# Layer norms of a one-layer encoder: transposes directly behind the normalisation, gain and bias applied per partition, rows of the residual scaled later

## The chip, the cores and the metric

The kernel runs on one core of a Trainium2 chip. The metric is the device time of one execution in microseconds (us). Engines are named as the profile names them: PE multiplies matrices (PEld loads its stationary operand), DVE works on tensors elementwise, ACT applies functions and copies, POOL does slow elementwise work and issues accumulating DMAs, SP issues the other DMAs. Each engine runs its own instructions in order and waits on semaphores of the others.

## The reference

One layer over 256 tokens of width 2048, all in float32:

```python
x = _layer_norm(ALPHA * x + 0.5 * _swiglu(x, ffn1_w1, ffn1_w3, ffn1_w2), ln1_g, ln1_b)
mix = _hybrid_mixer(x, w_in, b_gates_m, conv_m, norm_m, w_up_m, w_up_sb, w_out)
x = _layer_norm(ALPHA * x + mix, ln2_g, ln2_b)
x = _layer_norm(ALPHA * x + 0.5 * _swiglu(x, ffn2_w1, ffn2_w3, ffn2_w2), ln3_g, ln3_b)
x = x + sigmoid(x @ w_ple_gate) * (p @ w_ple_proj)
```

`_layer_norm` takes mean and variance over the 2048 columns of a token, and returns `(x - mu) * rsqrt(var + eps) * g + b`. The feed-forward width is 5632. The mixer is a projection to about 11,000 columns, two attention-like branches, gates and an output projection.

## The kernel before

Tokens stand in two halves, t = 0 and t = 1, of 128 rows each; the residual is kept as two tiles `xres0` and `xres1` of 128x2048. Products take activations transposed (columns on the partitions), in tiles `actT` for a chunk c of 512 columns and a half t. Every float32 operand is held as a rounded part and a remainder, and a product is three matmuls: rounded by rounded, rounded by remainder (of the weight), remainder (of the activation) by rounded. Lines 1061, 1062 and 1063 are those three; only the last needs the remainder of the activation.

Weights come in tiles of 256x512 (`raw`, 512 KB). ACT rounds each into `split` (L1010), DVE subtracts for the remainder (L1014). How many split tiles may exist at once is a number: 5 in the feed-forward stages, 6 in the mixer, and 11 around the borders between stages (`SPLIT_EDGE`, within `EDGE` tiles of a border). A **unit** is a weight tile used for one half t: six matmuls. Usually both halves use a tile one after the other. Around the three norms the order is skewed: the last `SKEW` tiles ahead of a norm are first used all for t = 0, then all for t = 1, and the first `SKEW` tiles behind it likewise. So a split tile lives until its unit of t = 1.

The engine orders are what this program emits, since it is written out by a small planner at build time: `sched.now` advances by each unit's matmul time, a generator spawned with a delay emits its instructions once the clock has passed, and nothing is reordered later. PSUM has a ring of six banks (`ps`) for products and transposes.

A norm goes so. A group's last unit adds its product to `xres` on DVE (L497 in the feed-forward stages, L875 in the mixer) and takes statistics of these 512 columns (L391). When all four are there, `finish` aggregates them (L397), takes the root on ACT and its reciprocal on DVE (L400), and for each chunk normalises (L404), multiplies by g (L406) and adds b (L407), both broadcast over the rows and held in four pages. `turn` follows 5.0 planner-us behind: four transposes on PE (L266), the rounding copy out of PSUM on ACT (L268), and the remainder on DVE (L274). For the second norm the kernel also keeps an unrounded copy (L273), from which `form_turn` builds sums for the next stage, and scales the rows by ALPHA on POOL (L421).

Of the kernel before, what the change touches and what calls it, by code (L numbers as in the profile page):

```python
# [21 lines left out]
ALPHA = 2.0 ** 0.25  # L22
EPS = 1e-5
COL = 512

PAGES = 44
TEMP_BUFS = 6
FORMED = 8
SPARE = 2
# [151 lines left out]
def kernel(  # L181
# [6 lines left out]
    nc = tc.nc  # L188
    x, out = x[0], out[0]
# [7 lines left out]
    small = ctx.enter_context(tc.tile_pool(name="small", bufs=4))  # L197
# [38 lines left out]
    def activate(out, in_, func, **kw):  # L236
        use_table(func)
        nc.scalar.activation(out, in_, func, **kw)  # L238
# [4 lines left out]
    ident = consts.tile([P, P], F32, name="ident")  # L243
# [6 lines left out]
    xres = [res_pool.tile([P, D], F32, name=f"xres{t}") for t in range(TT)]  # L250
# [8 lines left out]
    def split_psum(hi, lo, ps):  # L259
        nc.scalar.copy(hi, ps)  # L260
        nc.vector.tensor_tensor(out=lo, in0=ps, in1=hi, op=ALU.subtract)

    def transposed(src, act, c, t):
        ps = misc([P, 4, P])
        for k in range(4):
            nc.tensor.transpose(ps[:, k], src[:, k * P:(k + 1) * P], ident[:])  # L266
        dst = act.get(c, t)
        nc.scalar.copy(dst[:, 0], ps[:])  # L268
        if act.forms:
            if c not in act.whole:  # L270
                act.whole[c] = big()
                pages[0] += 1
            nc.scalar.copy(act.whole[c][:, t * COL:(t + 1) * COL], ps.rearrange("q k s -> q (k s)"))  # L273
        nc.vector.tensor_tensor(out=dst[:, 1], in0=ps[:], in1=dst[:, 0], op=ALU.subtract)  # L274
        act.mark(c, t, 4)
        if act.forms and all(act.ready(c, h) for h in range(TT)):
            sched.spawn(form_turn(act, c), DELAY["form"] + 3.0 * c)
# [95 lines left out]


    class Norm:
        def __init__(self, g, b, act, after):
            self.g_in, self.b_in, self.act, self.after = g, b, act, after
            self.stats, self.half = {}, {}

        def load(self):  # L380
            use_table(ACT.Sqrt)
            self.g, self.b = [big(), big()], [big(), big()]
            for k in range(2):
                ks = slice(k * 1024, (k + 1) * 1024)
                nc.sync.dma_start(out=self.g[k][:], in_=self.g_in[ks].partition_broadcast(P))
                nc.sync.dma_start(out=self.b[k][:], in_=self.b_in[ks].partition_broadcast(P))

        def chunk(self, t, c):
            if t not in self.stats:
# [5 lines left out]
        def finish(self, t):  # L395
            mv = small.tile([P, 2], F32, name="mv", tag="mv")
            nc.vector.bn_aggr(out=mv[:], in_=self.stats[t][:])  # L397
            rstd = small.tile([P, 1], F32, name="rstd", tag="rstd")
            activate(rstd[:], mv[:, 1:2], ACT.Sqrt, bias=eps[:, 0:1])
            nc.vector.reciprocal(out=rstd[:], in_=rstd[:])  # L400
            for c in range(4):
                xs = xres[t][:, c * COL:(c + 1) * COL]
                gs = slice((c % 2) * COL, (c % 2 + 1) * COL)
                nc.vector.tensor_scalar(out=xs, in0=xs, scalar1=mv[:, 0:1], scalar2=rstd[:, 0:1],  # L404
                                        op0=ALU.subtract, op1=ALU.mult)
                nc.vector.tensor_tensor(out=xs, in0=xs, in1=self.g[c // 2][:, gs], op=ALU.mult)  # L406
                nc.vector.tensor_tensor(out=xs, in0=xs, in1=self.b[c // 2][:, gs], op=ALU.add)  # L407
                sched.spawn(self.turn(t, c), DELAY["ln_turn"])
                yield DELAY["ln_step"]

        def turn(self, t, c):
            xs = xres[t][:, c * COL:(c + 1) * COL]
            transposed(xs, self.act, c, t)
            if self.after:
                yield DELAY["after"]
                self.after(xs)
            return
            yield

    def scaled(xs):  # L420
        nc.gpsimd.tensor_scalar(out=xs, in0=xs, scalar1=ALPHA, scalar2=None, op0=ALU.mult)  # L421
# [537 lines left out]
    splits = {}  # L959
    pos = {"load": 0, "split": 0, "at": 0, "raw": 0}  # L960

    def mixing():
        j = pos["split"]
        return any(-EDGE <= j - e < EDGE for e, _ in edges) or [m for e, m in edges if e <= j][-1:] == [True]

    def limits(j):

        if any(-EDGE <= j - e < EDGE for e, _ in edges):
            return RAW_EDGE, SPLIT_EDGE
        mixer = [m for e, m in edges if e <= j][-1:] == [True]  # L970
        return (RAW_MIX, SPLIT_MIX) if mixer else (RAW_FFN, SPLIT_FFN)
# [129 lines left out]
```

## Time and profile before

| | |
|---|---|
| median of three runs | 2219.58 us (2218.72 to 2219.68) |
| the profiled execution | 2219.43 us, of which the span of its instructions 2217.6 us |
| granted PE clock, mean | 0.998 |
| places of the norms in the span | about 690 to 720, 1400 to 1430, 2094 to 2125 us |

The span is what the hardware profiler saw from the first to the last instruction; 1.8 us of the time lie around it. A row of the timeline gives start, duration, engine, line, operation, output and inputs, shapes, and in brackets how long the engine stood still before it and what ended that. The view of waits adds these brackets up. A row of the windows gives, for a stretch of the span, its length and then the busy time and number of instructions of PE, PEld, DVE, ACT and POOL, the granted clock, the share of the DMA engines and GB/s. Rows of grouped instructions give shape, count, busy time in us and the mean of one in ns.

### The profile page before, as it was taken

The page shows a single profiled execution, that of the slowest core. Times are in us where ns is not written, and L with a number is a line of the kernel's source. Part 1 is how long each engine was busy: PE and PEld are TensorE (multiplying, and loading weights), DVE is VectorE, ACT ScalarE, POOL GpSimd, SP SyncE. Part 2 cuts the span into 40 slices and gives each one's busy share as a digit, 9 for nine tenths or more (in the row PEclk, how much of TensorE's full clock was granted, in tenths as well). Part 3 has the DMA queues.
Part 4 walks back from the last instruction along what each step waited for, and adds up shares of the span by engine and source line. Part 5 has one row for each costly group of instructions (what it writes and reads, how often), then busy time and mean ns, then how long its engine had stood idle before and what let it go on. Part 6 is the DMA issues. An engine that isn't in the chain of part 4 may idle for free.

```text
span 2217.6 us, 27467 instructions
## 1 busy us (share of the span) xinstructions
PE 2198.4 (99%) x10065; PEld 1822.2 (82%) x10065; DVE 1688.1 (76%) x1856; ACT 1236.2 (56%) x1441; POOL 201.4 (9%) x175
## 2 busy tenths in 40 slices
PE   9999999999999999999999999999999999999999
PEld 7888888888887888888888888788888888888878
DVE  6889988888799674654445456789898989889874
ACT  6556656666563655545643344466666666666452
POOL 3111011110100000100100000121011101110000
PEclk9999999999999999999999999999999999999999
DMA  9899889987991765655566666679879988899543
GB/s 346 219 255 269 252 249 288 276 247 215 271 363 55 224 182 170 181 170 163 161 188 185 189 224 219 228 171 284 252 235 246 306 253 250 243 276 301 188 160 96
DMA packets 262857, 501.83 MB, mean 226 GB/s; under 512 B 15745, under 2 KB 24769, under 8 KB 262721
## 3 DMA queue, kind: packets, MB, share of 16 engines
q1 hardware_dynamic: 227904, 432.95, 59.0%
q0 software_dynamic: 34816, 67.12, 16.9%
q8 instruction: 79, 1.29, 0.2%
q14 instruction: 58, 0.47, 0.1%
HBM read 497.91 MB, written 2.10 MB: 225 GB/s over the span
## 4 chain that ended last, share of the span: by engine, by line
PE 95%; DVE 3%; DMA 1%; issue 1%; ACT 0%; DVEq 0%; ACTq 0%
PE mm L1063 27%; PE mm L1062 27%; PE mm L1061 27%; PE seeded L1063 4%; PE seeded L1062 4%; PE seeded L1061 4%; PE ms L266 1%; DMA raw<-in_ffn_w_dram 1%; DVE xres L406 1%; DVE split L1014 0%; DVE xres L404 0%; DVE xres L407 0%; DVE actT L274 0%; DVE stats L391 0%; PE ms L772 0%
## 5 line engine op out<-in xcount | busy, mean ns | idle before, releaser
L1014 DVE TENSOR_TENSOR split<-raw,split 128x1024 fp32r<-128x1024 f32 (+1 forms) x1013 | 1181.1, 1202 | 302.1 <-ACT split L1010 289.5
L1010 ACT CAST split<-raw 128x1024 fp32r<-128x1024 f32 (+1 forms) x1013 | 1017.6, 1038 | 448.2 <-PE mm L1062 112.4
L1061 PE MATMUL mm<-split,actT 128*128 128x512 f32 (+2 forms) x2768 | 1076.5, 389 | 0.3 <-ACT split L1010 0.3
L1063 PE MATMUL mm<-split,actT 128*128 128x512 f32 (+2 forms) x2768 | 1066.4, 385 | 8.2 <-DVE actT L274 8.2
L1062 PE MATMUL mm<-split,actT 128*128 128x512 f32 (+2 forms) x2768 | 1065.5, 385 | 1.8 <-DVE split L1014 1.8
L1063 PEld LDWEIGHTS mm<-split,actT 128*128 128x128 f32 x2768 | 520.7, 188 | 115.0 <-DVE actT L274 11.4
L1062 PEld LDWEIGHTS mm<-split,actT 128*128 128x128 f32 x2768 | 521.2, 188 | 103.1 <-DVE split L1014 3.0
L1061 PEld LDWEIGHTS mm<-split,actT 128*128 128x128 f32 x2768 | 521.0, 188 | 102.2 <-issue 1.3
L330 POOL DMA_DIRECT2D raw<-in_ffn_w_dram x128 | 155.5, 1219 | 982.6 <-DVE split L1014 787.5
L335 DVE TENSOR_TENSOR raw<-raw 128x1024 f32<-128x1024 f32 x128 | 155.6, 1216 | 11.0 <-DMA raw<-in_ffn_w_dram 11.0
L1061 PE MATMUL seeded<-split,actT 128*128 128x512 f32 x384 | 150.5, 392 | 0.0
L1062 PE MATMUL seeded<-split,actT 128*128 128x512 f32 x384 | 149.6, 390 | 0.0
L1063 PE MATMUL seeded<-split,actT 128*128 128x512 f32 x384 | 149.5, 389 | 0.0
L497 DVE SCALAR_TENSOR_TENSOR xres<-mm,xres 128x512 f32<-128x512 f32 x160 | 108.4, 682 | 12.8 <-PE mm L1063 12.8
L268 ACT CAST actT<-ms 128x512 fp32r<-128x512 f32 x84 | 49.1, 588 | 113.8 <-PE ms L266 113.7
L1062 PEld LDWEIGHTS seeded<-split,actT 128*128 128x128 f32 x384 | 72.1, 188 | 15.0 <-DVE split L1014 0.4
L1063 PEld LDWEIGHTS seeded<-split,actT 128*128 128x128 f32 x384 | 72.1, 188 | 15.0
L1061 PEld LDWEIGHTS seeded<-split,actT 128*128 128x128 f32 x384 | 72.1, 188 | 14.7
L274 DVE TENSOR_TENSOR actT<-ms,actT 128x512 fp32r<-128x512 f32 x84 | 57.1, 684 | 30.0 <-ACT actT L268 17.7
L421 POOL TENSOR_SCALAR xres<-xres 128x512 f32<-128x512 f32 x16 | 27.0, 1692 | 325.2 <-DVE xres L404 300.5
L238 ACT ACTIVATE temp<-mm 128x512 f32<-128x512 f32 (+1 forms) x38 | 21.8, 574 | 58.0 <-PE mm L1063 58.0
L238 ACT ACTIVATE big<-mm 128x512 f32<-128x512 f32 x20 | 12.0, 598 | 55.8 <-PE mm L1063 55.8
(124 smaller groups left out, 630.6 us busy)
## 6 DMA issues: line engine op xcount, KB each, us to landing
raw<-in_ffn_w_dram SPq DMA_DIRECT2D x527, 512.0 KB, 8.0
raw<-in_w_in_dram SPq DMA_DIRECT2D x168, 512.0 KB, 3.7
raw<-in_ffn_w_dram POOLq DMA_DIRECT2D x128, 512.0 KB, 9.5
raw<-in_w_out_dram SPq DMA_DIRECT2D x32, 512.0 KB, 5.2
raw<-in_w_ple_gate_dram SPq DMA_DIRECT2D x24, 512.0 KB, 4.9
raw<-in_w_up_m_dram SPq DMA_DIRECT2D x16, 512.0 KB, 4.1
raw<-in_w_up_sb_dram SPq DMA_DIRECT2D x16, 512.0 KB, 4.1
raw<-in_w_ple_gate_dram SPq DMA_DIRECT2D x16, 256.0 KB, 4.6
```

The lines of the kernel that those rows point to most:

```text
L238: nc.scalar.activation(out, in_, func, **kw)
L268: nc.scalar.copy(dst[:, 0], ps[:])
L274: nc.vector.tensor_tensor(out=dst[:, 1], in0=ps[:], in1=dst[:, 0], op=ALU.subtract)
L330: nc.gpsimd.dma_start(out=raw.tile[:, :, :cols], in_=src.src, accum_op=ALU.add)
L335: nc.vector.tensor_tensor(out=a.tile[:, :, :cols], in0=a.tile[:, :, :cols], in1=b.tile[:, :, :cols], op=ALU.add)
L421: nc.gpsimd.tensor_scalar(out=xs, in0=xs, scalar1=ALPHA, scalar2=None, op0=ALU.mult)
L497: nc.vector.scalar_tensor_tensor(out=xs, in0=ps, scalar=0.5, in1=xs, op0=ALU.mult, op1=ALU.add)
L1010: nc.scalar.copy(hi[:, ks], r[:, ks])
L1014: nc.vector.tensor_tensor(out=lo[:, ks], in0=r[:, ks], in1=hi[:, ks], op=ALU.subtract)
L1061: nc.tensor.matmul(ps, hi, w[0][:, k, :u.cols], start=first, stop=False, skip_group_check=u.onto)
L1062: nc.tensor.matmul(ps, hi, w[1][:, k, :u.cols], start=False, stop=False, skip_group_check=u.onto)
L1063: nc.tensor.matmul(ps, lo, w[0][:, k, :u.cols], start=False, stop=last, skip_group_check=u.onto)
```

## The change

`finish` only normalises (L425, once L404), and emits the chunks 0.7 instead of 1.7 planner-us apart. `turn` comes 3.4 behind instead of 5.0: four transposes of the normalised rows (L434), and behind them g and b as scalars per partition, out of PSUM: one of the four 128x128 blocks on DVE (L439), three on ACT (through L238). The result, in SBUF, is then rounded on ACT (L260) and its remainder taken on DVE (L261). g and b per partition (`gb`) come from two small DMAs, one transpose and one copy (L405). The rows of the residual get g and b later, in `rows` (L460, L461, or L463 and L465 with ALPHA in them for the second norm, whose POOL scaling goes away), two DVE operations per chunk and half. `SKEW` and `EDGE` go from 6 to 8, the four broadcast pages are counted, and the rule for loading ahead looks at the split tiles that exist.

```diff
-EDGE = 6
+EDGE = 8
-SKEW = 6
+SKEW = 8
-    "after": 14.0, "form": 14.0, "ln_turn": 5.0, "ln_step": 1.7, "h": 8.0, "silu": 6.0, "late": 9.0, "rest": 1.2, "mt": 3.2,
+    "gb": 12.0, "form": 14.0, "ln_turn": 3.4, "ln_step": 0.7, "h": 8.0, "silu": 6.0, "late": 9.0, "rest": 1.2, "mt": 3.2,
         def load(self):
...
+            raw = temp()
+            n = D // P
+            nc.sync.dma_start(out=raw[0:n, 0:P], in_=self.g_in.rearrange("(c q) -> c q", q=P))
+            nc.sync.dma_start(out=raw[n:2 * n, 0:P], in_=self.b_in.rearrange("(c q) -> c q", q=P))
+            sched.spawn(self.columns(raw, n), DELAY["gb"])
...
                 nc.vector.tensor_scalar(out=xs, in0=xs, scalar1=mv[:, 0:1], scalar2=rstd[:, 0:1],
                                         op0=ALU.subtract, op1=ALU.mult)
-                nc.vector.tensor_tensor(out=xs, in0=xs, in1=self.g[c // 2][:, gs], op=ALU.mult)
-                nc.vector.tensor_tensor(out=xs, in0=xs, in1=self.b[c // 2][:, gs], op=ALU.add)
                 sched.spawn(self.turn(t, c), DELAY["ln_turn"])
         def turn(self, t, c):
-            xs = xres[t][:, c * COL:(c + 1) * COL]
-            transposed(xs, self.act, c, t)
-            if self.after:
-                yield DELAY["after"]
-                self.after(xs)
+            act = self.act
+            ps = misc([P, 4, P])
+            for k in range(4):
+                nc.tensor.transpose(ps[:, k], xres[t][:, (4 * c + k) * P:(4 * c + k + 1) * P], ident[:])
+            y = whole(act, c, t) if act.forms else temp()[:]
+            for k in (3, 0, 1, 2):
+                yk, gk, bk = y[:, k * P:(k + 1) * P], *(self.gb[:, i, 4 * c + k:4 * c + k + 1] for i in range(2))
+                if k == 3:
+                    nc.vector.tensor_scalar(out=yk, in0=ps[:, k], scalar1=gk, scalar2=bk, op0=ALU.mult, op1=ALU.add)
+                else:
+                    activate(yk, ps[:, k], ACT.Identity, scale=gk, bias=bk)
+            dst = act.get(c, t)
+            split_psum(dst[:, 0], dst[:, 1], y.rearrange("q (k s) -> q k s", s=P))
...
+            self.left -= 1
+            if self.left == 0:
+                sched.spawn(self.rows(), self.delay)
+        def rows(self):
+            for c in range(4):
+                for t in range(TT):
...
+                    if self.alpha is None:
+                        nc.vector.tensor_tensor(out=xs, in0=xs, in1=g, op=ALU.mult)
+                        nc.vector.tensor_tensor(out=xs, in0=xs, in1=b, op=ALU.add)
+                    else:
+                        nc.vector.scalar_tensor_tensor(out=xs, in0=xs, scalar=self.alpha, in1=g,
+                                                       op0=ALU.mult, op1=ALU.mult)
+                        nc.vector.scalar_tensor_tensor(out=xs, in0=b, scalar=self.alpha, in1=xs,
+                                                       op0=ALU.mult, op1=ALU.add)
+                    yield self.step
...
-    norm1 = Norm(ln1_g[0], ln1_b[0], x1T, None)
+    norm1 = Norm(ln1_g[0], ln1_b[0], x1T, None, 30.0, 6.0)
-    norm2 = Norm(ln2_g[0], ln2_b[0], x2T, scaled)
+    norm2 = Norm(ln2_g[0], ln2_b[0], x2T, ALPHA, 24.0, 5.0)
-    norm3 = Norm(ln3_g[0], ln3_b[0], x3T, None)
+    norm3 = Norm(ln3_g[0], ln3_b[0], x3T, None, 6.0, 2.6)
...
-               and (mixing() or pages[0] + pos["raw"] + 2 * limits(pos["split"])[1] < PAGES - SPARE)):
+               and (mixing() or pages[0] + pos["raw"] + 2 * max(limits(pos["split"])[1], len(splits)) < PAGES - SPARE)):
```

What this does to the engine orders is shown at the first norm; the other two read alike. First DVE before, from the first normalised chunk of t = 0 (`xres0`) on; `big` are the broadcast g and b, `mm` products, `ms` transposes.

```order
L404 TENSOR_SCALAR xres0_86<-xres0_86,mv_5821,rstd_5823 128x512
L406 TENSOR_TENSOR xres0_86<-xres0_86,big_5520 128x512
L407 TENSOR_TENSOR xres0_86<-xres0_86,big_5522 128x512
L1014 TENSOR_TENSOR split_5838<-raw_5556,split_5837 128x1024
L497 SCALAR_TENSOR_TENSOR xres1_87<-mm_5830,xres1_87 128x512
L391 BN_STATS stats_5770<-xres1_87 128x6
L404 TENSOR_SCALAR xres0_86<-xres0_86,mv_5821,rstd_5823 128x512
L406 TENSOR_TENSOR xres0_86<-xres0_86,big_5520 128x512
L407 TENSOR_TENSOR xres0_86<-xres0_86,big_5522 128x512
L497 SCALAR_TENSOR_TENSOR xres1_87<-mm_5856,xres1_87 128x512
```

And DVE of the changed kernel from the fourth normalised chunk of t = 0 on; `temp` is the transposed chunk with g and b, `gb` their values per partition.

```order
L425 TENSOR_SCALAR xres0_86<-xres0_86,mv_5800,rstd_5802 128x512
L439 TENSOR_SCALAR temp_5850<-ms_5845,gb_5668 128x128
L261 TENSOR_TENSOR actT_5855<-temp_5850,actT_5855 128x512
L1065 TENSOR_TENSOR split_5859<-raw_5559,split_5858 128x1024
L548 SCALAR_TENSOR_TENSOR xres1_87<-mm_5837,xres1_87 128x512
L413 BN_STATS stats_5828<-xres1_87 128x6
L439 TENSOR_SCALAR temp_5877<-ms_5872,gb_5668 128x128
L261 TENSOR_TENSOR actT_5882<-temp_5877,actT_5882 128x512
L1065 TENSOR_TENSOR split_5886<-raw_5581,split_5885 128x1024
L439 TENSOR_SCALAR temp_5903<-ms_5898,gb_5668 128x128
```

The broadcast g and b are gone from here. In their place each chunk has L439 and, directly behind it, L261; between the chunks stand splits of weight tiles (L1065, once L1014), of which the order before has one at this place. The adds and statistics of t = 1 stand behind them as before. From the add that completes `xres0` to the first normalised chunk of t = 1, DVE now has five splits, all four turns of t = 0, and four adds with statistics of t = 1, in this order.

ACT of the changed kernel at the same place, with the semaphores that each row waits for.

```order
L1061 CAST split_5831<-raw_5517 128x1024 [waits DMAHW5_49]
L238 ACTIVATE temp_5850<-ms_5845,gb_5668 128x128 [waits DVE_49]
L238 ACTIVATE temp_5850<-ms_5845,gb_5668 128x128 x2
L260 CAST actT_5855<-temp_5850 128x512 [waits Activation_49]
L1061 CAST split_5858<-raw_5559 128x1024 [waits DMAHW7_49]
L238 ACTIVATE temp_5877<-ms_5872,gb_5668 128x128 [waits DVE_49]
```

The first of the three ACTIVATEs of a chunk waits for DVE: for L439 of the same chunk, which reads the same PSUM bank. The CAST follows them, and L261 on DVE needs that CAST; the next weight tile's CAST stands behind it.

PE of the changed kernel where the first transpose of t = 1 stands: the end of the third unit behind the norm, and the fourth.

```order
L1114 MATMUL mm_5961<-split_5735,actT_5882 128x512 [waits DVE_49]
L1112 MATMUL mm_5961<-split_5735,actT_5882 128x512
L1113 MATMUL mm_5961<-split_5736,actT_5882 128x512
L1114 MATMUL mm_5961<-split_5735,actT_5882 128x512
L434 MATMUL ms_5983<-ident_82,xres1_87 128x128 [waits DVE_49]
L434 MATMUL ms_5983<-ident_82,xres1_87 128x128 x3
L1112 MATMUL mm_5961<-split_5815,actT_5882 128x512
L1113 MATMUL mm_5961<-split_5816,actT_5882 128x512
```

Between the last unit of `xres0` and this transpose PE has 8 units of t = 1, the four transposes of t = 0, and 3 units behind the norm. Before, the first transpose of t = 1 stood 4 units behind the norm, the last half having 6 units. The transpose waits for DVE's first L425 of t = 1, and every later PE row stands behind it.

More of the change, by code (lines that the diff above doesn't have):

```diff
@@ L269, in transposed, with whole, finished @@
         if act.forms:
[L270 to L273, printed above, removed]
+            nc.scalar.copy(whole(act, c, t), ps.rearrange("q k s -> q (k s)"))
         nc.vector.tensor_tensor(out=dst[:, 1], in0=ps[:], in1=dst[:, 0], op=ALU.subtract)
+        finished(act, c, t)
+    def whole(act, c, t):
+        if c not in act.whole:
+            act.whole[c] = big()
+            pages[0] += 1
+        return act.whole[c][:, t * COL:(t + 1) * COL]
+    def finished(act, c, t):
         act.mark(c, t, 4)
@@ L375, with __init__ @@
     class Norm:
-        def __init__(self, g, b, act, after):
-            self.g_in, self.b_in, self.act, self.after = g, b, act, after
-            self.stats, self.half = {}, {}
+        def __init__(self, g, b, act, alpha, delay, step):
+            self.g_in, self.b_in, self.act = g, b, act
+            self.alpha, self.delay, self.step = alpha, delay, step
+            self.stats, self.left = {}, 8
         def load(self):
@@ L382, in load @@
             self.g, self.b = [big(), big()], [big(), big()]
+            pages[0] += 4
             for k in range(2):
@@ L386, in load, with columns @@
                 nc.sync.dma_start(out=self.b[k][:], in_=self.b_in[ks].partition_broadcast(P))
+            raw = temp()
[3 more added lines that the diff above has]
+            sched.spawn(self.columns(raw, n), DELAY["gb"])
+        def columns(self, raw, n):
+            ps = misc([P, 2 * n])
+            nc.tensor.transpose(ps[:], raw[0:2 * n, 0:P], ident[0:2 * n, 0:2 * n])
+            self.gb = small.tile([P, 2, n], F32, name="gb", tag="gb", bufs=1)
+            nc.vector.tensor_copy(out=self.gb[:], in_=ps.rearrange("q (a c) -> q a c", c=n))
+            drop()
+            return
+            yield
         def chunk(self, t, c):
```

8 lines of the change are left out of this document (7 added, 1 removed).

## The prediction

> **What bounds the kernel now.** I read the page first, then PE's waits, then the windows around the norms, then the timelines of DVE and PE there.
>
> ```profile
> span 2217.6 us, 27467 instructions
> PE 2198.4 (99%) x10065; PEld 1822.2 (82%) x10065; DVE 1688.1 (76%) x1856; ACT 1236.2 (56%) x1441; POOL 201.4 (9%) x175
> PE mm L1063 <- DVE actT L274: 8.2, 7, 2.7
> PE ms L266 <- ACT split L1010: 2.2, 1, 2.2
> 690.00:720.00 30.00, 26.84 (x121) 21.24 (x120) 27.29 (x47) 5.90 (x10) 0.00 (x0) 0.94 0.18 46
> 1400.00:1430.00 30.00, 27.14 (x131) 21.54 (x131) 24.86 (x40) 9.70 (x19) 10.55 (x6) 1.00 0.61 216
> 2094.00:2125.00 31.00, 27.94 (x128) 22.16 (x127) 28.49 (x47) 12.26 (x22) 0.00 (x0) 0.94 0.36 103
> ```
>
> PE is busy for 99% of the span: whatever PE doesn't wait for costs nothing. Of its 19 us of idle time nearly half lies at the three norms (the windows, first number behind the length): 3.16, 2.86 and 3.06, together 9.1 us. In the first and third the granted clock is 0.94, which is another 0.06 x 26.84 = 1.6 and 0.06 x 27.94 = 1.7. So the norms cost **12.4 us now**, and that is the most that this change can win. DVE is busy for 27.29 of 30 there: it is DVE's queue that PE waits for.
>
> **The walk along DVE.** This is DVE at the first norm; 692.73 is the add that completes `xres0`, and PE ended that half's last matmul just before (call it T0).
>
> ```profile
> 692.73 0.69 DVE L497 SCALAR_TENSOR_TENSOR xres<-mm,xres 128x512 f32<-128x512 f32 x1 [1.16 <-PE mm L1063]
> 693.45 0.69 DVE L391 BATCH_NORM_STATS2 stats<-xres 128x6 f32<-128x512 f32 x1
> ...
> 694.80 0.16 DVE L400 RECIPROCAL rstd<-rstd 128x1 f32<-128x1 f32 x1 [0.36 <-ACT rstd L238]
> 695.00 0.55 DVE L404 TENSOR_SCALAR xres<-xres,mv,rstd 128x512 f32<-128x512 f32 x1
> 695.58 0.69 DVE L406 TENSOR_TENSOR xres<-xres,big 128x512 f32<-128x512 f32 x1
> 696.31 0.69 DVE L407 TENSOR_TENSOR xres<-xres,big 128x512 f32<-128x512 f32 x1
> 696.92 1.22 DVE L1014 TENSOR_TENSOR split<-raw,split 128x1024 fp32r<-128x1024 f32 x1
> 698.05 0.68 DVE L497 SCALAR_TENSOR_TENSOR xres<-mm,xres 128x512 f32<-128x512 f32 x1
> 698.77 0.69 DVE L391 BATCH_NORM_STATS2 stats<-xres 128x6 f32<-128x512 f32 x1
> 699.38 0.53 DVE L404 TENSOR_SCALAR xres<-xres,mv,rstd 128x512 f32<-128x512 f32 x1
> ```
>
> Start to start: add to first normalised chunk 2.27 (the head of a norm); a split 1.13; an add with its statistics 1.33; L406 and L407 together 1.34 a chunk, which the change takes off this place; a 128x512 operation that another follows 0.61. DVE stood idle for 1.16 ahead of T0, so it enters the norm without a backlog, and I assume the same behind the change.
>
> **What a turn costs DVE now.** A chunk had L274 here, 0.61 of DVE. The new turn is L439 and L261 next to each other, and between them lies ACT's whole part, because the first ACTIVATE waits for L439 and L261 waits for the CAST. No row shows L439, nor an ACTIVATE of 128x128 with two pointers out of PSUM; the nearest are these.
>
> ```profile
> L261 DVE TENSOR_TENSOR actT<-ms,actT 128x128 fp32r<-128x128 f32 x16 | 4.6, 290 | 14.8 <-ACT actT L260 14.8
> L238 ACT ACTIVATE temp<-ms,aT 128x128 f32<-128x128 f32 x4 | 1.4, 360 | 0.0
> L238 ACT ACTIVATE temp<-ms,cw 128x256 f32<-128x256 f32 x16 | 7.6, 474 | 18.4 <-DVE temp L671 14.6 <-PE ms L660 3.8
> L260 ACT CAST actT<-temp 128x512 fp32r<-128x512 f32 x16 | 9.3, 621 | 8.3 <-DVE split L1014 3.4 <-PE mm L1063 1.7 <-PE mm L1062 1.6
> 1112.03 0.27 ACT L260 CAST actT<-ms 128x128 fp32r<-128x128 f32 x1 [3.15 <-PE ms L795]
> 1112.33 0.29 DVE L261 TENSOR_TENSOR actT<-ms,actT 128x128 fp32r<-128x128 f32 x1 [2.00 <-ACT actT L260]
> 1112.65 0.43 ACT L260 CAST actT<-ms 128x128 fp32r<-128x128 f32 x2 [0.36 <-DVE actT L261]
> ```
>
> The hand-off between ACT and DVE is 1112.30 to 1112.33, so 0.03. I take 0.29 for L439; 3 x 0.36 = 1.08 for the ACTIVATEs (the row of the same engine, shape and source, without overlap, since theirs has one pointer operand less); 0.62 for the CAST; three hand-offs; 0.61 for L261: **2.69 us of DVE for a turn**. From below: ACTIVATEs that overlap like the two small CASTs, which take 0.43 together (0.16 + 0.16 + 0.27 = 0.59), with 0.21 for L439: about 2.1. From above: 3 x 0.474 = 1.42 and 0.46 for L439, an estimate at the length of half a chunk: about 3.2 with L261 at its full 0.69.
>
> [...]
>
> **The sum at an edge.** DVE from T0 to the end of the first normalised chunk of t = 1, by the changed order at the first norm: two heads 2 x 2.27 = 4.54; three more adds with statistics 3.99; four chunks of t = 0 normalised, 4 x 0.55 = 2.20; five splits 5.65; four turns 4 x 2.69 = 10.76; one chunk of t = 1, 0.55. Three of the splits start about 0.35 late, since their CAST (1.05 on ACT) only starts behind the turn's CAST, while DVE has 0.61 to do: 1.05. Together **28.7, with the first step from PE 28.8**.
>
> PE's way to the same point needs these rows.
>
> ```profile
> 690.03 0.39 PE L1062 MATMUL mm<-split,actT 128*128 128x512 f32 x1
> ...
> 691.39 0.39 PE L1062 MATMUL mm<-split,actT 128*128 128x512 f32 x1
> ...
> 716.89 0.44 PE ms L266 x4
> ```
>
> Six matmuls lie between the first two: a unit is 1.36. Four transposes take 0.44 on the chain. 8 units, 4 x 0.44, and 3 units make 10.88 + 1.76 + 4.08 = 16.7, less 0.16, because the next matmul starts while the last one still drains: 16.6 us behind T0. PE then waits for **28.8 - 16.6 = 12.2 us**, where its longest wait was 2.7. At the second norm a group's last column alone lies behind T0, so three adds with statistics are missing: 12.2 - 4.0 = 8.2. At the third the order is that of the first; PE has three units of another product at that place, whose PSUM banks come free with the turns, so part of the wait comes earlier, but the end is the same: 12.2. Together 32.6. Afterwards a turn of 2.69 keeps ahead of PE, which takes 2 x 1.36 + 0.44 for a chunk.
>
> **The clock after the wait.** This is what followed the wait of 2.70.
>
> ```profile
> 705.25 0.50 PE L1063 MATMUL mm<-split,actT 128*128 128x512 f32 x1 [2.70 <-DVE actT L274]
> ...
> 706.28 0.63 PE L1061 MATMUL mm<-split,actT 128*128 128x512 f32 x1
> 706.71 0.63 PE L1062 MATMUL mm<-split,actT 128*128 128x512 f32 x1
> ...
> 708.42 0.63 PE L1063 MATMUL mm<-split,actT 128*128 128x512 f32 x1
> 708.84 1.01 PE L266 MATMUL ms<-ident,xres 128*128 128x128 f32 x4
> ...
> 1.11 3.79 PE L949 MATMUL seeded<-ones 128*128 128x128 f32 x16 [1.11 <-DVE eps L247]
> ...
> 8.87 0.39 PE L1063 MATMUL mm<-split,actT 128*128 128x512 f32 x1
> ```
>
> Matmuls came 0.43 apart instead of 0.23 from 706.28 to 708.84, and the transposes behind them lost as much: 1.6 us. At the start of the span PE, cold, first keeps its full pace at 8.87, so at most half of 7.76 is lost there: 3.9. At the second norm, with waits up to 1.7, the granted clock stayed at 1.00. So the price behind a wait of 8 to 12 lies between 0 and 3.9; I take 2.5, between the two that are seen to lose: 7.5 us for three.
>
> [...]
>
> **What lies beside other work.** The rows of the residual are 16 operations a norm, 0.72 and 0.70 each: 11.3 us of DVE moved, not saved.
>
> ```profile
> L406 DVE TENSOR_TENSOR xres<-xres,big 128x512 f32<-128x512 f32 x24 | 17.3, 719 | 0.8
> L421 POOL TENSOR_SCALAR xres<-xres 128x512 f32<-128x512 f32 x16 | 27.0, 1692 | 325.2 <-DVE xres L404 300.5 <-PE ms L266 22.5 <-DVE actT L274 2.2
> 720.00:740.00 20.00, 20.00 (x127) 18.02 (x126) 12.40 (x19) 11.07 (x18) 0.00 (x0) 1.00 0.88 266
> 1460.00:1500.00 40.00, 40.00 (x182) 33.15 (x181) 30.68 (x31) 22.68 (x26) 4.81 (x4) 1.00 0.75 181
> 2125.00:2218.00 93.00, 88.03 (x481) 76.67 (x479) 46.55 (x60) 34.12 (x47) 0.00 (x0) 0.98 0.40 130
> ```
>
> In the mixer and at the end DVE has 38 to 50% free: 0. Behind the second norm it has 9.3 of 40, less than 11.3, with five splits ahead (13.6 us of PE) as cover: 0, and up to 2 if that is used up. The eight scalings on POOL that go (13.5 us) were behind nobody. The small DMAs, transpose and copy of `gb` lie 20 us ahead: 0. The DMA share at the norms is 0.18 to 0.61, so loading one tile less ahead costs nothing that I can see.
>
> **Sum.** 32.6 + 7.5 - 12.4 = +27.7. The profiled execution took 2219.43, of which 1.8 lie outside the span, and the median is 2219.58: **2247 us**. From below: turns of 2.1 take 2.4 off each edge (7.1), and no slow clock 7.5: 2232. From above: turns of 3.2 add 2.1 an edge, a clock as from cold 4.2, DVE behind the second norm 2: 2260. Range 2232 to 2260.
>
> **Rivals.** (1) L261 finds ACT's part done, so that a turn takes DVE 0.21 + 0.61 = 0.82 and no split is late. An edge is then 8.5 shorter: waits of 3.7, 0 and 3.7, and 1.6 of clock for two: 10.6 against 12.4, so 2217.6, **no change** (0.2%, or 4.4 us, is about what can be told from none). For it: ACT is busy for only 5.90 of 30 at this place. Against it: the order puts nothing between L439 and L261. (2) The first half's turns hide wholly beside the 8 units of t = 1, **faster**: all 12.4 go, 2207. The point is where DVE's sum falls under PE's 16.6. Without any time for turns it is 28.8 - 10.8 - 1.1 = 16.9, so the splits would also have to be done ahead of T0, in the idle 1.16 or so before each add. For it: the last two DVE operations in front of a transpose go, 1.34 a chunk. Against it: 11 split tiles, of which 8 are held by the skewed tail. (3) DVE falls behind in the feed-forward stage past its five splits: slower, over 2260.
>
> **Chances.** Forecast 0.86, (1) 0.06, (2) 0.05, (3) 0.03. Faster by over 0.2%: 0.05; within: 0.06; slower: 0.89.
>
> **What would show it.** PE's longest waits are at the first transpose of t = 1 (L434 for DVE's L425), about 12, 8 and 8 to 12; DVE waits for ACT `actT` at L261 by about 1.8 a turn, 24 times; the granted clock in the three windows is below 0.94. If DVE's wait at L261 is short, (1) holds; if L434 doesn't wait, (2). If the waits are as said and the time isn't, something elsewhere has gained, which I have not found.

## The result, and the profile after

The changed kernel takes **2245.26 us** (2244.39 to 2246.34, four runs) against 2219.15 beside it: 1.0118 of before, with a 95% interval of 1.010 to 1.0135. The profiled execution took 2244.72, 25.3 more than that of before. 2247 was forecast, with 2232 to 2260 as the range.

The same views as before, of the changed kernel: two lines of the page, then the view of PE's waits, then the windows around the three norms (the first number behind the length is PE's busy time).

```profile
span 2243.0 us, 27579 instructions
...
PE 2201.9 (98%) x10068; PEld 1824.6 (81%) x10068; DVE 1693.9 (76%) x1883; ACT 1262.8 (56%) x1505; POOL 187.3 (8%) x167
```

PE's waits (total, times, longest):

```profile
PE ms L434 <- DVE xres L425: 27.6, 3, 11.6
PE mm L1112 <- ACT temp L238: 3.3, 2, 2.7
```

The windows:

```profile
680.00:740.00 60.00, 48.23 (x217) 38.90 (x217) 35.21 (x58) 23.48 (x46) 0.00 (x0) 0.89 0.24 70
1400.00:1450.00 50.00, 41.49 (x194) 34.11 (x193) 22.74 (x39) 22.35 (x42) 0.00 (x0) 0.93 0.44 143
2094.00:2140.00 46.00, 35.09 (x160) 27.61 (x160) 33.31 (x53) 18.41 (x32) 0.00 (x0) 0.90 0.30 92
```

PE's share went from 99 to 98%, and DVE has 5.8 us more to do than the 1688.1 of before: by the sums of busy time little has happened. In the windows PE stands idle for 11.8, 8.5 and 10.9 us at the norms, 31.2 together, where it was 9.1 (3.16, 2.87 and 3.06 in these wider windows too). Three single waits carry most of it, at the first transpose of t = 1 (L434) for the first normalised chunk of t = 1 (L425). DVE is the engine waited for, and yet it is busy for only 35 of 60 us there. Its timeline at the first norm shows why.

```profile
690.67 0.69 DVE L548 SCALAR_TENSOR_TENSOR xres<-mm,xres 128x512 f32<-128x512 f32 x1 [1.30 <-PE mm L1114]
...
698.37 0.41 DVE L439 TENSOR_SCALAR temp<-ms,gb 128x128 f32<-128x128 f32 x1
700.65 0.69 DVE L261 TENSOR_TENSOR actT<-temp,actT 128x512 fp32r<-128x512 f32 x1 [1.88 <-ACT actT L260]
701.61 1.23 DVE L1065 TENSOR_TENSOR split<-raw,split 128x1024 fp32r<-128x1024 f32 x1 [0.26 <-ACT split L1061]
...
704.08 0.40 DVE L439 TENSOR_SCALAR temp<-ms,gb 128x128 f32<-128x128 f32 x1
706.35 0.69 DVE L261 TENSOR_TENSOR actT<-temp,actT 128x512 fp32r<-128x512 f32 x1 [1.88 <-ACT actT L260]
...
719.28 1.92 DVE L425 TENSOR_SCALAR xres<-xres,mv,rstd 128x512 f32<-128x512 f32 x4
```

The bracket of 1.88 us stands at L261 in every turn: DVE does its block, and then stands still for ACT's three blocks and the CAST. ACT has the other side of it.

```profile
698.81 1.16 ACT L238 ACTIVATE temp<-ms,gb 128x128 f32<-128x128 f32 x3 [4.21 <-DVE temp L439]
700.00 0.62 ACT L260 CAST actT<-temp 128x512 fp32r<-128x512 f32 x1
700.53 1.05 ACT L1061 CAST split<-raw 128x1024 fp32r<-128x1024 f32 x1
```

ACT had been idle for 4.21 us when it was let go by L439 at 698.78. So a turn is a **ring of two queues**: ACT may not start before DVE has come to L439, and DVE may not go on before ACT has finished. PE finds out at 719.88, in this timeline of its chunks of t = 1 at the same norm (a chunk is four transposes and a unit), with the last wait at the third norm below it.

```profile
719.88 1.12 PE L434 MATMUL ms<-ident,xres 128*128 128x128 f32 x4 [11.58 <-DVE xres L425]
...
723.36 0.96 PE L434 MATMUL ms<-ident,xres 128*128 128x128 f32 x4
...
725.55 0.60 PE L434 MATMUL ms<-ident,xres 128*128 128x128 f32 x4
...
727.38 0.60 PE L434 MATMUL ms<-ident,xres 128*128 128x128 f32 x4
...
2139.37 1.11 PE L434 MATMUL ms<-ident,xres 128*128 128x128 f32 x4 [7.54 <-DVE xres L425]
```

Behind the wait two chunks take PE 725.55 - 719.88 = 5.67, where an undisturbed one takes 1.83: 2.0 us went to slow matmuls. The same sum gives 1.3 at the second norm and 2.2 at the third. At the third PE also waits for PSUM banks (0.57 and 2.71) ahead of the wait shown, and the last three of the six matmuls between that 2.71 and the 7.54 already begin 0.40 and 0.43 apart, not 0.23 (2130.37, 2130.77 and 2131.20): another 0.6. So the norms cost 31.2 + 6.1 = 37.3 us now, 24.9 more than the 12.4 of before; of the 25.3 between the two profiled executions 0.4 is left that I don't place.

### The profile page after: what moved, and what is told of

The parts are those of the page before. It is cut to its first block, busy times and chain, and to the rows that moved or that the text cites. A ratio compares the mean times of both kernels' runs of the same rounds, so it can differ in the third digit from the quotient of the medians.

```text
span 2243.0 us, 27579 instructions
## 1 busy us (share of the span) xinstructions
PE 2201.9 (98%) x10068; PEld 1824.6 (81%) x10068; DVE 1693.9 (76%) x1883; ACT 1262.8 (56%) x1505; POOL 187.3 (8%) x167
## 4 chain that ended last, share of the span: by engine, by line
PE 95%; DVE 2%; ACT 1%; DMA 1%; issue 1%; DVEq 0%
PE mm L1112 27%; PE mm L1114 27%; PE mm L1113 27%; PE seeded L1113 4%; PE seeded L1112 4%; PE seeded L1114 4%; PE ms L266 1%; DVE split L1065 1%; DMA raw<-in_ffn_w_dram 1%; ACT temp L238 0%; PE ms L434 0%; ACT split L1061 0%; DVE xres L548 0%; DVE stats L413 0%; PE ms L823 0%
## 5 line engine op out<-in xcount | busy, mean ns | idle before, releaser
L1065 DVE TENSOR_TENSOR split<-raw,split 128x1024 fp32r<-128x1024 f32 (+1 forms) x1013 | 1183.5, 1202 | 294.2 <-ACT split L1061 276.0
L548 DVE SCALAR_TENSOR_TENSOR xres<-mm,xres 128x512 f32<-128x512 f32 x160 | 108.5, 683 | 15.6 <-PE mm L1114 15.6
L268 ACT CAST actT<-ms 128x512 fp32r<-128x512 f32 x60 | 35.1, 587 | 68.7 <-PE ms L266 65.1
L271 DVE TENSOR_TENSOR actT<-ms,actT 128x512 fp32r<-128x512 f32 x60 | 40.9, 684 | 24.1 <-ACT actT L268 13.8
L238 ACT ACTIVATE temp<-mm 128x512 f32<-128x512 f32 (+1 forms) x38 | 21.8, 574 | 52.6 <-PE mm L1114 52.6
L261 DVE TENSOR_TENSOR actT<-temp,actT 128x512 fp32r<-128x512 f32 x32 | 21.4, 688 | 32.7 <-ACT actT L260 32.7
L434 PE MATMUL ms<-ident,xres 128*128 128x128 f32 x96 | 16.7, 303 | 27.6 <-DVE xres L425 27.6
```

The lines of the kernel that those rows point to most:

```text
L548: nc.vector.scalar_tensor_tensor(out=xs, in0=ps, scalar=0.5, in1=xs, op0=ALU.mult, op1=ALU.add)
L1065: nc.vector.tensor_tensor(out=lo[:, ks], in0=r[:, ks], in1=hi[:, ks], op=ALU.subtract)
```

## The experiments

Theory A is the ring: DVE's way from T0 to t = 1 is long because it waits inside each turn for an ACT that could have begun earlier. Theory B: the turn is slow because of its operations, whoever starts them and wherever they stand. Two more parts of the change are in question by themselves: the longer skew, and the rows. Ratios are against the kernel before on the same chip, which took 2219.2 to 2219.8.

| run | time, us | ratio, 95% interval |
|---|---|---|
| the change | 2245.26 | 1.0118 (1.010 to 1.0135) |
| e1, all blocks on ACT | 2215.91 | 0.9983 (0.9974 to 0.9992) |
| e2, L261 later | 2243.88 | 1.0110 (1.0096 to 1.0123) |
| e3, DVE's block in its own bank | 2230.43 | 1.0049 (1.0036 to 1.0062) |
| e4, all blocks on DVE | 2243.05 | 1.0104 (1.009 to 1.0118) |
| e5, transposes of t = 1 later | 2235.93 | 1.0074 (1.0062 to 1.0087) |
| e6, skew of 6 | 2235.22 | 1.0071 (1.0059 to 1.0084) |
| e7, before, with a skew of 8 | 2225.44 | 1.0027 (1.0016 to 1.0037) |
| e8, without the rows | 2244.74 | 1.0114 (1.0099 to 1.013) |
| e9, e1 and e5 together | 2205.96 | 0.9938 (0.9924 to 0.9951) |
| e10, e1 with a skew of 6 | 2208.98 | 0.9951 (0.9939 to 0.9964) |
| e11, e1, e5 and a skew of 6 | 2208.06 | 0.9948 (0.9935 to 0.996) |
| e12, own bank, and DVE rounds its block | 2221.37 | 1.0011 (1.0002 to 1.002) |

### e1: the ring opened

```diff
-                if k == 3:
-                    nc.vector.tensor_scalar(out=yk, in0=ps[:, k], scalar1=gk, scalar2=bk, op0=ALU.mult, op1=ALU.add)
-                else:
-                    activate(yk, ps[:, k], ACT.Identity, scale=gk, bias=bk)
+                activate(yk, ps[:, k], ACT.Identity, scale=gk, bias=bk)
```

> All four blocks of a turn on ACT, none on DVE (no L439). Theory A: a turn is a ring, DVE to ACT to DVE: ACT may not start before DVE's L439, DVE stands 1.88 us at L261 until ACT is done, and every later operation of DVE stands behind that. Without L439 ACT starts when PE's transposes are there and DVE meanwhile does splits and adds. DVE's way at the first norm (29.2 us in the changed kernel, 690.67 to 719.82) loses 4 x (0.41 + 1.88) and about 0.8 of late splits: 19.3 against PE's 17.6. Waits of PE at the first transpose of t = 1 fall from 11.6, 8.5 and 7.5 to 0 to 3 each; DVE's wait at L261 nearly goes; time 2211 to 2221 us. Rival B: the turn is slow because of its operations (ACTIVATEs of 454 ns), whoever starts it: with one more of them on ACT the waits stay within 1 us of what they are, and the time at 2242 to 2249.

2215.91: one small block moved from DVE to ACT takes 29 us off. First PE's waits, then DVE at the first norm, then ACT, in this run.

```profile
PE ms L434 <- DVE xres L425: 8.2, 3, 2.9
```

```profile
697.70 0.68 DVE L261 TENSOR_TENSOR actT<-temp,actT 128x512 fp32r<-128x512 f32 x1
...
709.01 1.92 DVE L425 TENSOR_SCALAR xres<-xres,mv,rstd 128x512 f32<-128x512 f32 x4
```

```profile
697.53 1.50 ACT L238 ACTIVATE temp<-ms,gb 128x128 f32<-128x128 f32 x4
699.06 0.62 ACT L260 CAST actT<-temp 128x512 fp32r<-128x512 f32 x1
```

No bracket is left at L261 of t = 0: ACT, which has more to do than in the changed kernel, is a whole chunk ahead of DVE. DVE's way goes from its add at 690.00 (to 709.55, the end of the first of the four chunks), 19.6 where it was 29.2. The waits are 2.80, 2.46 and 2.89, since PE arrives after 16.8 here, not after 17.6. Theory A holds and B falls: ACT has four blocks of a turn instead of three, and the time went down.

### e2: L261 behind the next split

```diff
-            split_psum(dst[:, 0], dst[:, 1], y.rearrange("q (k s) -> q k s", s=P))
+            nc.scalar.copy(dst[:, 0], y.rearrange("q (k s) -> q k s", s=P))
+            yield 1.4
+            nc.vector.tensor_tensor(out=dst[:, 1], in0=y.rearrange("q (k s) -> q k s", s=P), in1=dst[:, 0], op=ALU.subtract)
```

> The changed kernel with L261 of each turn emitted one unit of PE (1.36 us) later, behind the next split; L439 stays. Theory A, in its strict form (it is the place of L261 that costs): DVE no longer stands at L261, 1.88 x 4 come off each edge, time about 2218. Theory A, as a ring of queues: on ACT the CAST of the next split stands behind the turn's CAST, so DVE's split, which now stands where L261 stood, waits for ACT instead, until about 2.8 us behind L439 (698.78 to 701.58 at the first norm); PE then waits for the later L261 as well as for the transposes, the sum of the waits stays at about 31, and the time within 3 us of 2245. I hold the second for the likelier.

2243.88, so the second reading in the time. DVE at the first norm, and two of PE's waits:

```profile
697.90 0.41 DVE L439 TENSOR_SCALAR temp<-ms,gb 128x128 f32<-128x128 f32 x1
701.13 1.23 DVE L1067 TENSOR_TENSOR split<-raw,split 128x1024 fp32r<-128x1024 f32 x1 [2.82 <-ACT split L1063]
...
707.95 0.68 DVE L445 TENSOR_TENSOR actT<-temp,actT 128x512 fp32r<-128x512 f32 x1
```

```profile
PE ms L434 <- DVE xres L425: 12.6, 3, 7.3
PE mm L1116 <- DVE actT L445: 9.9, 4, 4.9
```

The late L445 no longer waits, but the split in its old place waits longer (2.82), because its own CAST stands on ACT behind the turn's. PE's wait is now split between the transposes and the first matmul that needs the remainder. The waits at the norms are 26.6 in all, 4.5 less, where I had expected about 31, so the sum of that reading was wrong by as much; there are more of them, though, and at the first norm three stretches with matmuls 0.43 apart follow them (from 709.28, 715.71 and 720.49) in place of one. Putting work between the two halves of a ring helped little here, because that work hangs on the same queue.

### e3 and e12: the shared bank, and what else closes the ring

```diff
-            for k in range(4):
-                nc.tensor.transpose(ps[:, k], xres[t][:, (4 * c + k) * P:(4 * c + k + 1) * P], ident[:])
+            own = misc([P, P])
+            for k in (3, 0, 1, 2):
+                nc.tensor.transpose(own[:] if k == 3 else ps[:, k], xres[t][:, (4 * c + k) * P:(4 * c + k + 1) * P], ident[:])
...
-                    nc.vector.tensor_scalar(out=yk, in0=ps[:, k], scalar1=gk, scalar2=bk, op0=ALU.mult, op1=ALU.add)
+                    nc.vector.tensor_scalar(out=yk, in0=own[:], scalar1=gk, scalar2=bk, op0=ALU.mult, op1=ALU.add)
```

> The block that DVE takes is transposed into a PSUM tile of its own (a second bank for each turn, of six in all); the operations and their order stay. So the first ACTIVATE no longer waits for L439, and DVE keeps its 0.41 for each. Theory A: ACT is done when DVE gets to L261 wherever DVE comes late; an edge loses 4 x 1.88 and some 0.8 of late splits, waits of about 3, 0 to 1 and 3, time 2213 to 2224, some us above the run with all blocks on ACT (4 x 0.41 at each edge), and PE may wait for PSUM banks. Rival B: as the changed kernel less 4 x 0.41 at each edge, 2239 to 2243. [...]

2230.43, outside both ranges: 15 us gained where theory A had 21 to 32. ACT at the first norm, then DVE:

```profile
694.57 1.16 ACT L238 ACTIVATE temp<-ms,gb 128x128 f32<-128x128 f32 x3 [0.58 <-PE ms L435]
698.24 0.62 ACT L260 CAST actT<-temp 128x512 fp32r<-128x512 f32 x1 [2.52 <-DVE temp L440]
```

```profile
697.75 0.41 DVE L440 TENSOR_SCALAR temp<-ms,gb 128x128 f32<-128x128 f32 x1
698.89 0.69 DVE L261 TENSOR_TENSOR actT<-temp,actT 128x512 fp32r<-128x512 f32 x1 [0.74 <-ACT actT L260]
```

The ACTIVATEs of this chunk now start 3.2 us ahead of DVE's block, as soon as the transposes are there (those of the other three 1.3 to 2.6 ahead). But the CAST takes the whole chunk, DVE's block with it, and so waits 2.52 for L440; 0.74 of the 1.88 (the CAST and its hand-offs) is left in each turn. I had overlooked that second way through which the ring closes. To see if it is the rest, DVE also rounds its own block:

```diff
-            split_psum(dst[:, 0], dst[:, 1], y.rearrange("q (k s) -> q k s", s=P))
+            yb = y.rearrange("q (k s) -> q k s", s=P)
+            nc.scalar.copy(dst[:, 0, 0:3], yb[:, 0:3])
+            nc.vector.tensor_copy(out=dst[:, 0, 3], in_=yb[:, 3])
+            nc.vector.tensor_tensor(out=dst[:, 1], in0=yb, in1=dst[:, 0], op=ALU.subtract)
```

> As the run with a bank for DVE's block, and DVE also makes the rounded half of that block itself; ACT's CAST takes its own three blocks (128x384) and no longer waits for DVE. In that run DVE still stood 0.74 at L261 of each turn and 0.26 at the split behind it, since the CAST of the whole chunk waited for DVE's block. Theory: that was the rest of the ring; 4 x 0.74 + 3 x 0.26 go and 4 copies of 0.2 to 0.3 come: some 2.7 less at each edge, waits at the first transpose of t = 1 of about 2.1, 0 to 1 and 2 in place of 4.8 and less, time 2219 to 2224. Rival: PE's waits for PSUM banks (4.2 in all in that run) and the slow clock carry the difference: 2227 to 2231.

2221.37, as the theory has it; the profiled execution, 2219.36, is the fastest of eleven. DVE in this run, then PE's waits for L425:

```profile
698.16 0.41 DVE L440 TENSOR_SCALAR temp<-ms,gb 128x128 f32<-128x128 f32 x1
698.61 0.23 DVE L446 CAST actT<-temp 128x128 fp32r<-128x128 f32 x1
698.93 0.69 DVE L447 TENSOR_TENSOR actT<-temp,actT 128x512 fp32r<-128x512 f32 x1
```

```profile
PE ms L435 <- DVE xres L425: 7.5, 3, 3.0
```

DVE keeps a block of its own and doesn't stand still in the turns of t = 0 any more. PE's waits at L435 for L425 are 3.0, 1.5 and 3.0, where I had expected 2.1, 0 to 1 and 2; two tiles of PSUM for a turn also cost PE 1.6 of small waits at the first norm and 1.6 at the third. So the shared bank and the shared CAST together make the ring (e3 gives the block a PSUM tile of its own together with the bank, so which of the two had ordered the engines is not parted), and cutting both brings the time from 2245 to 2221 with all of the work still done, and by the same engines but for the CAST of that block.

### e4: all blocks on DVE

```diff
-                if k == 3:
-                    nc.vector.tensor_scalar(out=yk, in0=ps[:, k], scalar1=gk, scalar2=bk, op0=ALU.mult, op1=ALU.add)
-                else:
-                    activate(yk, ps[:, k], ACT.Identity, scale=gk, bias=bk)
+                nc.vector.tensor_scalar(out=yk, in0=ps[:, k], scalar1=gk, scalar2=bk, op0=ALU.mult, op1=ALU.add)
```

> All four blocks of a turn on DVE, none on ACT (no ACTIVATE); CAST on ACT and L261 on DVE stay, so the ring stays, and DVE works where it waited. Theory A: DVE's turn is four blocks (0.41, then by 0.2 to 0.35 more each), hand-off, CAST 0.62, hand-off, L261 0.61: 2.3 to 2.7 us against 2.89 in the changed kernel, so an edge is 0.8 to 2.4 shorter; waits of 9 to 11, 6 to 8 and 8 to 10, time 2236 to 2243. Rival B (ACT's ACTIVATEs are the price): 3 x 0.35 of each turn go and little comes in their place, four turns an edge: 2230 to 2235.

2243.05, at the very edge of theory A's range (2243) and far outside B's. DVE at the first norm, then PE's waits:

```profile
698.20 1.36 DVE L438 TENSOR_SCALAR temp<-ms,gb 128x128 f32<-128x128 f32 x4
700.30 0.69 DVE L261 TENSOR_TENSOR actT<-temp,actT 128x512 fp32r<-128x512 f32 x1 [0.74 <-ACT actT L260]
```

```profile
PE ms L434 <- DVE xres L425: 27.0, 3, 11.2
```

A turn is 1.36 + 0.74 + 0.61 = 2.71 of DVE against 2.89: 0.7 less at an edge where I had 0.8 to 2.4. DVE works where it waited, and the longest wait of PE is still 11.2: what counts for PE is how long a turn holds DVE's queue, not whether DVE is busy in it.

### e5: the transposes of t = 1 two units later

```diff
-                sched.spawn(self.turn(t, c), DELAY["ln_turn"])
+                sched.spawn(self.turn(t, c), DELAY["ln_turn"] + 2.8 * t)
```

> The changed kernel with the transposes of t = 1 two units of PE (2 x 1.36 us) further back in PE's order; DVE's and ACT's work and order as before. Theory: the waits are DVE's way (29.2) less PE's way (17.6) to the same point, so each falls by 2.7: about 8.9, 5.8 and, at the third norm, 8 in all; 2.7 x 3 = 8 less: 2237 us (2234 to 2240). Rival: what PE waits for is the turns themselves, so that the wait only moves to the first unit of t = 1: 2243 to 2247.

2235.93, 9.3 less than the change. PE's waits in this run:

```profile
PE ms L434 <- DVE xres L425: 15.5, 3, 7.2
PE mm L1112 <- ACT temp L238: 3.9, 3, 2.7
...
PE mm L1112 <- DVE xres L548: 2.0, 2, 1.8
...
PE mm L1112 <- ACT actT L260: 1.1, 1, 1.1
```

22.5 in all against 31.1: 3.3, 2.7 and 2.7 off the three norms, where two units are 2.7, as DVE's way less PE's way gives it. At the third norm more of the wait now lies at the PSUM banks ahead of the transposes (L238 and L548, 5.7 together), and 2.45 at the transposes themselves.

### e6 and e7: the longer skew by itself

```diff
-EDGE = 8
+EDGE = 6
...
-SKEW = 8
+SKEW = 6
```

> The changed kernel with the lengths of the skewed part of before (6 units where the change has 8, at both sides of the norm). Between T0 and the first L425 of t = 1 DVE has one split in place of five; PE has 2 units less. Theory: DVE's way loses 4 x 1.14 + 0.76 = 5.3 (and 1.3 more, if an add falls ahead of T0), PE's way 2.7; the waits fall by 2.6 to 3.9 each, to about 8.5, 5 and 7.5; time 2234 to 2238. So the longer skew, taken alone, costs some 10 of the 25 us. Rival: the skew gives PE cover, and without it the waits grow by 2.7 each: 2253.

And the other way round, in the kernel before: 6 to 8 in both, with the changed rule for loading ahead.

> The kernel before with only the longer skew (8 units, and the limits of the change that go with it); norms as before. Theory: the tail holds 8 of 11 split tiles, so four more splits fall between T0 and t = 1, 4 x 1.14 = 4.6 of DVE against 2 x 1.36 = 2.7 of PE: 1.8 worse at each norm, 5 in all, 2222 to 2227. Rival: the longer skew is cover for PE, 2.7 a norm: 2212 to 2215.

2235.22 and 2225.44: the longer skew costs 10 us of the change, and 6 by itself in the kernel before. PE's waits in e6, then in e7:

```profile
PE ms L434 <- DVE xres L425: 20.8, 3, 8.2
```

```profile
PE ms L266 <- DVE xres L407: 15.6, 9, 2.8
```

In e6 DVE's way is 22.1 (693.46 to 715.57 in its timeline) instead of 29.2, and PE's 15.0 (to 708.45, where its wait of 7.18 begins) instead of 17.6. In e7 PE waits at nine transposes for rows that the norm hasn't finished, 15.6 us, where its idle time at the norms was 9.1. Two units more give PE 2.7 of cover, and the four splits that they push into DVE's way take 4.6; in the changed kernel late splits and one more add come with them, 7.1 in all (29.2 less 22.1).

### e8: the rows left out

```diff
-                sched.spawn(self.rows(), self.delay)
+                pages[0] -= 4
```

> The changed kernel without the later scaling of the residual's rows by g and b (16 operations of DVE at each norm are left out, 11.3 us each time; so g, b and, at the second norm, the factor of the residual are missing from the output). Theory: they lie where DVE has time, at 0: 2244 to 2246. Rival: behind the second norm and in the mixer they push splits back; then 2240 or less.

2244.74, 0.5 from the change, with ranges that overlap: the 33 us of DVE for the rows (48 operations) cost nothing that can be told. This kernel leaves out g, b and, at the second norm, the factor of the residual.

### e9, e10 and e11: better than both

e9 has the edits of e1 and e5, e10 those of e1 and e6, e11 all three.

> All four blocks of a turn on ACT, and the transposes of t = 1 two units of PE further back. In the run with the blocks on ACT alone PE waits 2.80, 2.46 and 2.89 at the first transpose of t = 1; two units are 2.72, so the waits go and with them the slow clock behind them (about 1 us at the second norm and 2 at the third): 2215.9 less 8.2 less 2 to 3, time 2204 to 2208 us, faster than before by 0.5 to 0.7%. Rival: the first unit of t = 1 then waits for its turn, which takes ACT 2.05 and DVE 0.61 after the transposes, and half comes back: 2210 to 2213.

> All four blocks of a turn on ACT, and the skewed part 6 units long as before the change; so beside before this is the move of g and b alone, without the ring. Theory: in place of five splits one stands between T0 and t = 1, 4 x 1.14 less of DVE against 2 x 1.36 less of PE, 1.8 better than with 8 units, and one add with statistics (1.33) falls ahead of T0: waits of 0 instead of 2.5 to 2.9, time 2205 to 2210. Rival: with less cover the turns of t = 0 come late to PE: 2214 to 2218.

> Both: all blocks on ACT, 6 units, the transposes of t = 1 two units further back. Theory: nothing is left to win at the norms, so within 2 us of the better of the other two; the first unit of t = 1 then stands 2 units behind its transposes in place of 4, which a turn of ACT 2.05 and DVE 0.61 just fills (2.72): 2205 to 2210. Rival: the cover of 2 units is too short, some us slower than with 6 units and the transposes in place.

2205.96, 2208.98 and 2208.06, all inside their ranges. e9 is 13.8 us faster than before. In e10 PE still waits at the first transposes of t = 1, 0.83, 0.85 and 0.93, where I had expected nothing; taking these away as well wins e11 0.9 over e10, with ranges that overlap, and it stays 2.1 behind e9, where I had expected at most 2. The page's line on the engines in e9, then its windows at the norms:

```profile
PE 2194.0 (100%) x10068; PEld 1820.4 (83%) x10068; DVE 1685.0 (76%) x1859; ACT 1268.9 (58%) x1529; POOL 187.4 (9%) x167
```

```profile
680.00:740.00 60.00, 59.91 (x329) 51.52 (x328) 40.66 (x65) 33.62 (x67) 0.00 (x0) 1.00 0.45 139
1390.00:1430.00 40.00, 40.00 (x194) 33.11 (x193) 22.42 (x32) 26.66 (x53) 0.00 (x0) 1.00 0.59 191
2084.00:2140.00 56.00, 55.91 (x263) 46.08 (x262) 45.08 (x62) 41.31 (x72) 0.00 (x0) 1.00 0.43 128
```

PE is idle for 0.2 us at the three norms together, and the granted clock is 1.00: there is nothing left there. The runs also part the change into pieces, in us against before on the same chip: everything but the skew of 8 and DVE's block, that is g and b off DVE's way to the transposes and all of them on ACT, with the later rows, the delays and the rule for loading ahead, -10.8 (e10); the longer skew, +7.2 (e1 is at -3.6); one block of four on DVE, +29.7 (the change is at +26.1). The last two steps are one edit each; the pieces of the first, but for the rows (e8), were not tried by themselves.

## Why the prediction was right, step by step

- **What the norms could give.** 12.4 us was called the most that the change can win. e9, which takes out all waits at the norms, wins 13.8; so the bound was near, 1.4 too small. The change itself wins nothing of it.
- **The turn.** Forecast 2.69 us of DVE, serial; measured 2.89 (698.37 to 701.26, that is 700.65 + 0.61). The mechanism was as said, and two terms were small: L439 took 0.41 and not 0.29, and the ACTIVATEs 1.16 and not 1.08. The row that I took had one pointer operand, theirs have two: 454 ns against 360. The three of a turn take 1.16 together, less than 3 x 0.454 = 1.36: they start 0.36 apart (698.81 and 699.17) and overlap.
- **The edge.** DVE's way was 28.8 by forecast and 29.2 in the trace: 0.8 more for the turns, 0.3 less for the late splits (0.26, 0.25 and 0.25, not 0.35 each). PE's way was 16.6 by forecast and 17.6 in the trace, some of it pauses at 703.58, where it waits 0.19 for a bank, and at 707.10. So the wait was 11.6, not 12.2. That it comes so near is partly luck: both ways were taken too short, by 0.4 and 1.0, and a wait is their difference.
- **The second and third norm.** 8.2 and 12.2 by forecast, 8.5 and 10.8 in the trace, at the third 0.57 and 2.71 of it at the PSUM banks of another product, as foreseen, and 7.54 at the transposes. DVE's way at the third is 29.2 again (2110.16 to 2139.31); what was too short is PE's, 16.6 by forecast and 18.3 without its waits, 0.6 of it the slow matmuls ahead of the last wait. The waits add up to 31.1 against 32.6.
- **The clock.** 7.5 by forecast for the three, 6.1 measured. For its size this is the term that was most wrong. The 2.5 for each wait was put between 1.6, which the rows behind a wait show, and 3.9, which rests on an estimate that half of the first 7.76 us is lost; no run shows that loss, and the rows behind the waits show 2.0, 1.3 and 2.2. 27.7 was forecast between the two executions; less 1.5 for the waits, less 1.4 for the clock, and with the 0.4 that I don't place, it is the 25.3 measured, but for rounding.
- **Behind the wait.** The sentence that PE takes 2 x 1.36 + 0.44 for a chunk there was wrong: in the trace a chunk is one unit and takes 1.83 (725.55 to 727.38), less than a turn. It cost nothing: PE's waits list none for a turn of t = 1 behind the three transposes.
- **The rows.** Costed at 0; e8 shows 0.
- **The longer skew.** Its splits were in DVE's sum (5.65 and 1.05); e6 shows by their removal that they were rightly there. I did not say that the skew by itself costs more than it covers, which e7 shows without the new turns.
- **The rivals.** (1), L261 finds ACT done, was priced at 2217.6; where e1 makes it so (and has no L439, so a turn takes DVE 0.61 and not 0.82), 2215.9 is measured. But what I gave as the reason against it, that nothing stands between L439 and L261, was not enough: e2 puts a split there and gains 1.4. (2), all turns hidden, was priced at 2207; e9 gets there, by another way than I named, with all blocks on ACT and more of PE's work ahead of the transposes instead of the splits ahead of T0.
- **The bank.** The turn was added up as L439, then ACT, then L261, and so it ran in the changed kernel. With a bank of its own for DVE's block (e3) ACT doesn't start beside L439, it starts 1.3 to 3.2 us ahead of it, and the time falls to 2230. So the order of the two engines on the shared tile and bank cost this kernel not the 0.41 of one read but the coupling of two queues. That two engines read one bank at once was not tried.

## What to carry to other kernels

Sharing one small job between two engines to balance them ties their queues together: look for every point at which each waits for the other, and let the one that is waited for least do the whole of it, even if it then has more to do. When an engine that is far from busy is waited for, read its timeline for brackets between two halves of one job, and ask what stands behind them; moving one half won next to nothing here, since what came in between hung on the same partner. A longer skew is cover for one engine and work for another: count both, here 2.7 against 4.6 to 7.1.

## What the runs showed of the hardware

In these runs what is lost behind a wait of PE doesn't grow with the wait. In the changed kernel 2.0, 1.3 and 2.2 us were lost behind waits of 11.6, 8.5 and 7.5 (ahead of the last one PE was already slow, behind a wait of 2.71); in e1, whose PE timeline has these rows at the three norms, waits of a quarter to two fifths of that lost as much or more, or nothing.

```profile
709.61 0.66 PE L434 MATMUL ms<-ident,xres 128*128 128x128 f32 x4 [2.80 <-DVE xres L425]
...
711.49 0.60 PE L434 MATMUL ms<-ident,xres 128*128 128x128 f32 x4
...
1416.48 0.66 PE L434 MATMUL ms<-ident,xres 128*128 128x128 f32 x4 [2.46 <-DVE xres L425]
...
1418.82 1.05 PE L434 MATMUL ms<-ident,xres 128*128 128x128 f32 x4
...
2111.55 1.08 PE L434 MATMUL ms<-ident,xres 128*128 128x128 f32 x4 [2.89 <-DVE xres L425]
...
2115.00 1.05 PE L434 MATMUL ms<-ident,xres 128*128 128x128 f32 x4
```

The third chunks begin at 713.31, 1421.77 and 2118.02, so two chunks took 3.7, 5.3 and 6.5 us, where 3.65 is undisturbed: 0, 1.6 and 2.8 lost. In e12 two waits of the same length, 3.04 at the first norm and 3.02 at the third, lost 0.1 and 1.6. At the second norm of e1 the matmuls first kept their pace and slowed 1.5 us after the wait. So the length of a wait doesn't say what is lost behind it: 2.80 lost nothing, 2.46 and 2.89 lost 1.6 and 2.8. What decides it these runs don't show.

The granted clock of a window with long waits can't be turned into lost time: at the first norm of the changed kernel 0.89 of 48.23 would make 5.3 us, and the rows show 2.0. Before, with shorter waits, the same product gave 1.6 and 1.7 at the first and third norm, and the rows show 1.6 at both.
